# A two-layer decoder trunk on one Trainium2 core: rstd moved from the FFN's input to its outputs, one more hidden-column group as Strassen block products, and down projections issued in halves behind each group

## The chip, the cores and the metric

The kernel runs on one core of one Trainium2 chip. The metric is device time in microseconds (us), from the start of the execution to its end. The kernel before the change takes 994.29 us, the median of 3 runs that lie between 994.14 and 994.36.

Engines are named as in the profile: PE is TensorE (matrix products; PEld is its loading of the stationary operand), DVE is VectorE, ACT is ScalarE, POOL is GpSimd, and SP is SyncE, which issues most of the transfers.

## What is computed

The input is a sequence of 512 positions with 1024 channels, in float32. Two layers follow each other; each has a mixer (its own kind in each layer) and a gated FFN, both on an RMS-normalized input and added to the residual. A last RMSNorm ends the trunk. The change concerns the two FFNs:

```python
def gated_conv_ffn(x, w_gate, w_up, conv_w, conv_b, w_down):
    g = jnp.einsum('bsd,df->bsf', x, w_gate)
    g = causal_dwconv3(g, conv_w) + conv_b
    up = jnp.einsum('bsd,df->bsf', x, w_up)
    return jnp.einsum('bsf,fd->bsd', jax.nn.silu(g) * up, w_down)
...
hn = rms_norm(h, norm_ffn[layer])
h = h + gated_conv_ffn(hn, w_ffn_gate[layer], w_ffn_up[layer], ...)
```

The hidden width is 2816, so there are 22 tiles of 128 hidden columns. `rms_norm` multiplies each position by rstd, the reciprocal root of its mean square, and each channel by a gain. As rstd belongs to the position alone, it may be applied to the FFN's input or to the products of gate and up.

## The kernel before

**Number format.** Every float32 operand of a matrix product is split into two parts, hi (rounded) and lo (the rest). A product is three matmuls into one PSUM bank: hi·hi, hi·lo and lo·hi (`mm3`, L152 to 155). The split of a weight chunk costs an ACT copy (hi) and a DVE subtraction (lo) in `parts` (L145 to 150), or, in `summed` (L136 to 143), an ACT copy of the negated data into lo, an accumulating transfer issued by POOL that adds the hi/lo remainder, and another ACT copy.

**Stages.** mixer0, ffn0 (L777), mixer1 (L795), ffn1 (L1059). Channels stand on partitions and positions run along the free axis. The kernel is written for a Tile scheduler that orders the instructions of each engine by itself and allocates buffers from pools: raw weights have 4 buffers, hi and lo of weights 6 each, the tag "sum" 3, the activations 4 each, and PSUM has 7 banks for products.

**The FFN's hidden part.** The 22 tiles are worked through in groups of two (f = 0, 2, ..., 20).
- Group 0 (`direct`, L592) multiplies the weights by h times gain, which isn't normalized yet, because rstd is only being worked out beside it. `evacuate` (L609) multiplies rstd into the gate's rows (L615, DVE) and into the silu's result s (L618, POOL). It is 2 tiles × (gate, up) × 8 k-chunks × 3 = 96 matmuls of 512 columns.
- When rstd is known, `normalize` (L626) forms x = h · gain · rstd for each pair of k-chunks (L631, DVE), splits it into hi and lo again (L635 ACT, L636 DVE), and forms the block sums t23 and t41 that the block products need (L643 to L646), with their splits.
- Group 2 is direct too, on the normalized input: again 96 matmuls of 512 columns.
- Groups 4 to 20 (`both`, L681) compute gate and up with Strassen-Winograd block products: the two tiles of columns, the two halves of the 1024 channels and the two halves of the 512 positions form 2×2 blocks, and seven products replace eight. The weights' sums are s12 and s34 (L698 to L707). That is 14 products (7 for gate, 7 for up) × 4 k-chunks × 3 = 168 matmuls of 256 columns (L535). `after` (L727 and on) copies product blocks into the rows of the gate (`rows`) and into `kept` for up, or adds them there.
- Then each tile has its causal convolution (an ACT copy at L564 and two DVE SCALAR_TENSOR_TENSOR at L566), silu (L572, ACT), the product with up (L750, L751, L754, DVE) and the split into a_hi (L260, ACT) and a_lo (L262, DVE) for the down projection.

**The down projection.** `PARTS` (L516) sets the order: after groups 0 and 2 a part over tiles 0 and 1; after group 4 one over tiles 2 to 5; from there on two groups in a row and then a part over four tiles (6 to 9, 10 to 13, 14 to 17, 18 to 21), over all 1024 output columns. So each part of four tiles covers the newest group and the one before it. In layer 0 `project` (L286) does two halves of 512 output columns with the weights as stationary operand and adds into h (L305, DVE). In layer 1 `down` (L1145) has the activations as stationary operand and adds into the token-major residual y (L1109, DVE). The last part of layer 1 is followed by the final norm and the output transfers.

## Time and profile before

| what | value |
|---|---|
| median of 3 runs | 994.29 us (994.14 to 994.36) |
| the profiled execution | 994.15 us |
| its span | 992.4 us |
| granted TensorE clock, mean | 0.998 |
| instructions | 14934 |
| transfers | 125.07 MB, 126 GB/s over the span |

How to read the rows that follow in the prediction: the page's first part gives busy time, share of the span and number of instructions of each engine. A row of a group is: line, engine, operation, out<-in by name, partitions × elements and type, count | busy us, mean ns of one | idle us of the engine just before them and what ended most of it. A row of the timeline is: start, length (us), engine, line, operation, and in brackets the idle time before it with what released it. A row of the chain is: start, length, what. A row of the windows view is a stretch of the span with its length, then the busy time of each engine, the granted clock, the share of the transfer engines and GB/s. Matmuls overlap: the time that one takes from TensorE is its distance to the next one's start, and not its length.

### The profile page before, as it was taken

To read this page: it belongs to the slowest core of one execution; us is meant where nothing else is said; L and a number is where in the kernel's file an instruction comes from. 1 tells how busy PE (TensorE), PEld (TensorE's weight loads), DVE (VectorE), ACT (ScalarE), POOL (GpSimd) and SP (SyncE) were. 2 spreads that over 40 slices of the span, in tenths; PEclk is the share of its full clock that TensorE was granted. 3 is DMA by queue.
4 is the path that set the end of the run, shared out by engine and by line. 5 is a ranking of instruction groups with operands and counts; after the bars stand their busy time and mean duration, and the time that the engine had idled before them with its cause. 6 is when DMAs were issued, how large, how long until landed. Compare 5 with 4: busy or idle time off the path is not lost.

```text
span 992.4 us, 14934 instructions
## 1 busy us (share of the span) xinstructions
PE 982.9 (99%) x5905; PEld 875.6 (88%) x5905; DVE 728.5 (73%) x1104; ACT 536.3 (54%) x806; POOL 105.3 (11%) x121
## 2 busy tenths in 40 slices
PE   9999999999999999999999999999999999999997
PEld 6788888898999989999888988888989899898996
DVE  6897458967785877858988665399668768687676
ACT  5623346744653746537668634675546366363664
POOL 2141031200000000000300001211000010000100
PEclk9999999999999999999999999999999999999999
DMA  7442225544553645536423513435546456464542
GB/s 246 133 146 85 86 88 131 121 148 118 133 147 97 181 121 132 148 98 180 136 87 93 182 54 97 105 91 130 143 101 159 124 125 173 94 163 126 123 112 85
DMA packets 83073, 125.07 MB, mean 126 GB/s; under 512 B 4308, under 2 KB 56252, under 8 KB 83004
## 3 DMA queue, kind: packets, MB, share of 16 engines
q1 hardware_dynamic: 74028, 98.24, 31.4%
q0 software_dynamic: 7056, 23.60, 13.3%
q10 hardware_dynamic: 1920, 2.30, 0.7%
q8 instruction: 46, 0.75, 0.3%
q14 instruction: 23, 0.19, 0.1%
HBM read 98.42 MB, written 2.10 MB: 101 GB/s over the span
## 4 chain that ended last, share of the span: by engine, by line
PE 94%; issue 1%; DVE 1%; DMA 1%; ACT 0%; DVEq 0%; POOLq 0%; ACTq 0%
PE d L154 4%; PE d L153 4%; PE d L155 4%; PE dn L153 4%; PE dn L154 4%; PE dn L155 4%; PE gu L153 3%; PE gu L154 3%; PE gu L155 3%; PE v L153 1%; PE oo L155 1%; PE oo L153 1%; PE v L155 1%; PE oe L155 1%; PE oe L154 1%; PE v L154 1%
## 5 line engine op out<-in xcount | busy, mean ns | idle before, releaser
L153 PE MATMUL dn<-whi_dn,a_hi 128*128 128x512 f32 (+1 forms) x180 | 69.4, 386 | 0.0
L154 PE MATMUL dn<-wlo_dn,a_hi 128*128 128x512 f32 (+1 forms) x180 | 69.3, 385 | 0.0
L154 PE MATMUL d<-a_lo,whi_d 128*128 128x512 f32 x176 | 68.7, 390 | 0.0
L155 PE MATMUL d<-a_hi,wlo_d 128*128 128x512 f32 x176 | 68.5, 389 | 0.0
L155 PE MATMUL dn<-whi_dn,a_lo 128*128 128x512 f32 (+1 forms) x180 | 67.9, 385 | 0.0
L153 PE MATMUL d<-a_hi,whi_d 128*128 128x512 f32 x176 | 66.9, 390 | 0.0
L566 DVE SCALAR_TENSOR_TENSOR c<-rows,prm,c 128x512 f32<-128x512 f32 x88 | 66.4, 766 | 0.0
L141 POOL DMA_DIRECT2D wlo_g<-raw_g x22 | 19.1, 867 | 373.9 <-ACT wlo_g L140 257.9
L1109 DVE TENSOR_TENSOR y<-dn,y 128x512 f32<-128x512 f32 (+1 forms) x49 | 32.5, 674 | 23.3 <-PE dn L155 23.0
L140 ACT ACTIVATE wlo_g<-raw_g 128x1024 fp32r<-128x1024 f32 x22 | 23.2, 1056 | 42.4 <-PE dn L154 42.4
L572 ACT ACTIVATE s<-c,prm 128x512 f32<-128x512 f32 x44 | 31.7, 720 | 20.5 <-DVE c L566 20.4
L679 DVE TENSOR_TENSOR wlo_s34u<-s34u,whi_s34u 128x1024 fp32r<-128x1024 f32 x18 | 22.0, 1225 | 27.9 <-ACT whi_s34u L678 27.9
L155 PEld LDWEIGHTS dn<-whi_dn,a_lo 128*128 128x128 f32 x180 | 33.8, 188 | 7.3 <-DVE a_lo L262 0.2
L678 ACT ACTIVATE whi_s12u<-s12u 128x1024 fp32r<-128x1024 f32 x18 | 18.9, 1051 | 39.3 <-PE d L154 33.7
L153 PEld LDWEIGHTS dn<-whi_dn,a_hi 128*128 128x128 f32 x180 | 33.8, 188 | 7.0 <-ACT a_hi L260 0.2
L154 PEld LDWEIGHTS dn<-wlo_dn,a_hi 128*128 128x128 f32 x180 | 33.8, 188 | 6.4
L154 PEld LDWEIGHTS d<-a_lo,whi_d 128*128 128x128 f32 x176 | 33.1, 188 | 7.3 <-DVE a_lo L262 0.2
L305 DVE TENSOR_TENSOR h<-d,h 128x512 f32<-128x512 f32 x48 | 32.5, 683 | 9.2 <-PE d L155 9.2
L153 PEld LDWEIGHTS d<-a_hi,whi_d 128*128 128x128 f32 x176 | 32.8, 188 | 7.0
L155 PEld LDWEIGHTS d<-a_hi,wlo_d 128*128 128x128 f32 x176 | 33.0, 188 | 6.7
L260 ACT ACTIVATE a_hi<-s 128x512 fp32r<-128x512 f32 x44 | 27.6, 628 | 16.1 <-DVE s L751 7.4
L149 DVE TENSOR_TENSOR wlo_dn<-raw_dn,whi_dn 128x1024 fp32r<-128x1024 f32 x22 | 26.8, 1220 | 11.6 <-ACT whi_dn L148 11.6
(1274 smaller groups left out, 3469.1 us busy)
## 6 DMA issues: line engine op xcount, KB each, us to landing
raw_g<-in_w_ffn_gate_dram SPq DMA_DIRECT2D x36, 512.0 KB, 4.6
raw_u<-in_w_ffn_up_dram SPq DMA_DIRECT2D x36, 512.0 KB, 4.7
wlo_g<-raw_g POOLq DMA_DIRECT2D x22, 512.0 KB, 4.7
raw_d<-in_w_ffn_down_dram SPq DMA_DIRECT2D x22, 512.0 KB, 4.0
raw_dn<-in_w_ffn_down_dram SPq DMA_DIRECT2D x22, 512.0 KB, 4.0
wlo_u<-raw_u POOLq DMA_DIRECT2D x19, 512.0 KB, 4.6
raw_oe<-in_w_out_even_dram SPq DMA_DIRECT2D x8, 512.0 KB, 3.6
raw_g<-in_w_ffn_gate_dram SPq DMA_DIRECT2D x16, 256.0 KB, 2.9
```

What stands on the lines that cost most here:

```text
L140: first = nc.scalar.activation(lo, raw, AF.Copy, scale=-1.0)
L141: nc.gpsimd.dma_start(lo, raw, accum_op=ALU.add)
L149: behind(nc.vector.tensor_tensor(lo, raw, hi.bitcast(F32), ALU.subtract), after[0])
L153: nc.tensor.matmul(ps, lhs[0], rhs[0], start=start, stop=False)
L154: nc.tensor.matmul(ps, lhs[0], rhs[1], start=False, stop=False)
L155: nc.tensor.matmul(ps, lhs[1], rhs[0], start=False, stop=stop)
L260: nc.scalar.activation(hi, src, AF.Copy, scale=scale)
L305: nc.vector.tensor_tensor(h[k], ps, h[k], ALU.add)
L566: nc.vector.scalar_tensor_tensor(c, t[:, i : S + i], prm("cf", i * NF + ft), c, op0=ALU.mult, op1=ALU.add)
L572: nc.scalar.activation(s, c, AF.Silu, bias=self.prm("bf", ft))
L679: nc.vector.tensor_tensor(lo, src, hi.bitcast(F32), ALU.subtract)
L1109: nc.vector.tensor_tensor(dst, ps, dst, ALU.add)
```

## The change

The input of the FFN is no longer normalized in either layer. `normalize` is replaced by `block_sums`, which forms t23 and t41 from h times gain with no rstd in it, so it no longer waits for rstd; hg stays the un-normalized split that group 0 uses. Group 2 goes through `both` like the groups behind it. In `both`, rstd multiplies the gate's rows ahead of the convolution (DVE, in both layers), and in layer 0 also s[1] and the first two blocks of kept. In layer 1 the up half's rstd is applied in the y-add behind the down projection, as a column of four positions' scalars (`self.cols`). Group 0's multiplication of s by rstd moves from POOL to DVE in layer 0 and is dropped in layer 1.

`PARTS` gives way to `STEPS`: after group 2 comes the part of tiles 0 and 1, and after each group from 4 on half a down part, 512 output columns of a part of four tiles: behind group 4 the first half of tiles 2 to 5, behind group 6 its second half, behind group 8 the first half of tiles 6 to 9, and so on; behind group 20 both halves of tiles 18 to 21. In the steps marked late (True), the split of the group's activations is issued behind the half part. Finally `summed` takes a function `between`, with which `both` issues the split of s12 behind the negated copy and the accumulating transfer of the second weight half.

The core of the diff:

```diff
-    def summed(raw, a, b, name):
+    def summed(raw, a, b, name, between=lambda: None):
...
         first = nc.scalar.activation(lo, raw, AF.Copy, scale=-1.0)
         nc.gpsimd.dma_start(lo, raw, accum_op=ALU.add)
+        between()
         behind(nc.scalar.activation(hi, raw, AF.Copy), first)
...
-    PARTS = (((0, 2), 0, 2), ((4,), 2, 6), ((6, 8), 6, 10), ((10, 12), 10, 14),
-             ((14, 16), 14, 18), ((18, 20), 18, 22))
+    STEPS = [(0, False, []), (2, False, [(0, 2, 0), (0, 2, 1)]), (4, False, [(2, 6, 0)])]
+    for f in range(6, NF - 2, 4):
+        STEPS += [(f, True, [(f - 4, f, 1)]), (f + 2, False, [(f, f + 4, 0)])]
+    STEPS[-1][2].append((NF - 4, NF, 1))
...
+            self.cols = small[:, 3 * PAD : 3 * PAD + NT]
...
                 for j in range(2):
                     t = padded_tile()
-                    if normed:
-                        nc.scalar.copy(t[:, 2:], banks[j])
-                    else:
-                        nc.vector.tensor_tensor(t[:, 2:], banks[j], r, ALU.mult)
-                    s = self.silu(self.conv(t, f + j), f + j)
-                    if not normed:
-                        nc.gpsimd.tensor_tensor(s, s, r, ALU.mult)
+                    nc.vector.tensor_tensor(t[:, 2:], banks[j], r, ALU.mult)
+                    s = self.silu(self.conv(t, j), j)
+                    if layer == 0:
+                        nc.vector.tensor_tensor(s, s, r, ALU.mult)
...
-        def normalize(self, kp):
-
-            n, r = f"{self.layer}_{kp}", self.r
-            x = self.ap.tile([P, 2, S], F32, tag="sum", bufs=3, name=f"x{n}")
-            for i, k in enumerate((kp, kp + NP)):
-                nc.vector.scalar_tensor_tensor(x[:, i, :], h[k], self.prm("ffn", k), r,
-                                               op0=ALU.mult, op1=ALU.mult)
...
-            halves(hg[kp], x[:, 0, :])
-            halves(hg[kp + NP], x[:, 1, :])
...
+        def block_sums(self, kp):
+
+            n, g1, h1 = f"{self.layer}_{kp}", self.prm("ffn", kp + NP), h[kp + NP]
             t = self.ap.tile([P, 4, HALF], F32, tag="sum", bufs=3, name=f"t{n}")
-            nc.vector.tensor_tensor(t[:, 1, :], b22, b12, ALU.subtract)
+            b11, b12 = t[:, 2, :], t[:, 3, :]
+            nc.scalar.activation(t[:, 2:, :], h[kp].rearrange("p (a b) -> p a b", a=2), AF.Copy,
+                                 scale=self.prm("ffn", kp))
+            nc.vector.scalar_tensor_tensor(t[:, 1, :], h1[:, HALF:], g1, b12, op0=ALU.mult,
+                                           op1=ALU.subtract)
             nc.vector.tensor_tensor(t[:, 0, :], t[:, 1, :], b11, ALU.add)
-            nc.vector.tensor_tensor(t[:, 3, :], b12, b11, ALU.subtract)
-            nc.vector.tensor_tensor(t[:, 2, :], b21, t[:, 0, :], ALU.subtract)
+            nc.vector.tensor_tensor(b12, b12, b11, ALU.subtract)
+            nc.vector.scalar_tensor_tensor(b11, h1[:, :HALF], g1, t[:, 0, :], op0=ALU.mult,
+                                           op1=ALU.subtract)
...
                 w = self.unit(f"s12{key}_{n}")
-                self.halves(*w, s12)
+
+                def split_s12():
+                    self.halves(*w, s12)
+
+                hi, lo = summed(*raws[key, 1], between=split_s12)
...
-                hi, lo = summed(*raws[key, 1])
...
-                if (key, product) == ("g", 4):
-                    s[1] = self.silu(self.conv(pads[1], f + 1), f + 1)
-                elif (key, product) == ("g", 3):
-                    s[0] = self.silu(self.conv(pads[0], f), f)
+                if (key, product) in (("g", 4), ("g", 3)):
+                    j = product == 4
+                    row = pads[j][:, 2:]
+                    nc.vector.tensor_tensor(row, row, self.r, ALU.mult)
+                    s[j] = self.silu(self.conv(pads[j], f + j), f + j)
+                    if j and layer == 0:
+                        nc.vector.tensor_tensor(s[1], s[1], self.r, ALU.mult)
...
+            if layer == 0:
+                nc.vector.tensor_tensor(kept[:, :2, :], kept[:, :2, :],
+                                        self.r.rearrange("p (a b) -> p a b", a=2), ALU.mult)
...
-            elif f == 2:
-                self.direct(2, True, ((0, 1), (2, 3)), self.ch)()
             else:
-                self.both(f)
+                rows = self.both(f)
+
+            def split_acts():
+                for ft, row in rows:
+                    self.act(ft, row)
+
+            return split_acts
...
+            for f, late, down_parts in STEPS:
+                acts = ffn.hidden(f)
+                if not late:
+                    acts()
+                for a, b, half in down_parts:
...
+                    project(f"d0_{a}", w_ffn_down[0], ffn.acts, list(range(a, b)), nxt,
+                            halves=(half,))
+                if late:
+                    acts()
...
+            def add(dst, ps, t):
+                nc.vector.scalar_tensor_tensor(dst, ps, ffn.cols[:, t : t + 1], dst,
+                                               op0=ALU.mult, op1=ALU.add)
...
+            for f, late, down_parts in STEPS:
+                splits = ffn.hidden(f, before=before)
+                if not late:
+                    splits()
+                if f == NF - 2:
+                    last_down(NF - 4, NF)
+                    break
+                for part in down_parts:
+                    half_down(*part)
+                if late:
+                    splits()
```

`half_down` is the layer-1 counterpart of `project` for one half: weights of 512 output columns as the moving operand, the activations as the stationary one, and `add` at the end of each bank. `last_down` is the former last part of layer 1, with `add` for the plain addition.

120 lines of the change are left out of this document (57 added, 63 removed).

## The prediction

> **What bounds the kernel now.** I read the profile's table of engines first, then the chain that ended last.
>
> ```profile
> span 992.4 us, 14934 instructions
> ...
> PE 982.9 (99%) x5905; PEld 875.6 (88%) x5905; DVE 728.5 (73%) x1104; ACT 536.3 (54%) x806; POOL 105.3 (11%) x121
> ...
> PE 94%; issue 1%; DVE 1%; DMA 1%; ACT 0%; DVEq 0%; POOLq 0%; ACTq 0%
> ```
>
> TensorE (PE) is busy for 99% of the span, and 94% of the chain is its own work. So a change gains what it takes off TensorE's list of matmuls, and loses each microsecond for which TensorE waits for DVE, ACT or a transfer. Next I read the windows over FFN layer 0: group 0, group 2, the first down part (two tiles), group 4, and group 4's down part (four tiles).
>
> ```profile
> core 0: us, PE busy (x) PEld busy (x) DVE busy (x) ACT busy (x) POOL busy (x), PEclk, DMA share, GB/s
> 146.10:169.30 23.20, 23.20 (x109) 19.22 (x108) 17.12 (x33) 14.19 (x22) 3.98 (x4) 1.00 0.56 137
> 169.30:191.10 21.80, 21.80 (x98) 18.04 (x97) 20.58 (x34) 16.39 (x27) 6.46 (x6) 1.00 0.46 97
> 191.10:202.00 10.90, 10.90 (x50) 9.03 (x49) 10.90 (x17) 6.12 (x7) 0.87 (x1) 1.00 0.53 144
> 202.00:222.10 20.10, 20.10 (x169) 20.10 (x168) 11.41 (x17) 11.17 (x18) 0.86 (x1) 1.00 0.48 136
> 222.10:243.90 21.80, 21.80 (x98) 17.93 (x97) 18.02 (x29) 8.02 (x10) 0.86 (x1) 1.00 0.52 141
> ```
>
> No window holds idle TensorE time, at full clock (1.00). The DVE column is the one to keep: 20.58 of 21.80 us in group 2, where `normalize` runs, and all of the 10.90 us behind it. DVE is close behind TensorE here, and the change gives DVE new work.
>
> **The change part by part.**
>
> *Group 2 from direct to block products (both layers).* It removes 96 matmuls of 512 columns a layer and adds 168 of 256. Matmuls overlap, so a row's length is no price; I take start to start, by the timeline (group 2's first matmul, the first of the down part behind it) and by the chain (runs of 12 block matmuls).
>
> ```profile
> 169.32 0.39 PE L153 MATMUL gu<-hgh,whi_g 128*128 128x512 f32 x1
> ...
> 191.08 0.39 PE L153 MATMUL d<-a_hi,whi_d 128*128 128x512 f32 x1
> ...
> 203.55 1.44 PE u_4a L535 x12
> 204.99 1.44 PE g_4e L535 x12
> ```
>
> Direct: 191.08 − 169.32 = 21.76 us, or 0.2267 each. Block: 14 runs of 1.44 = 20.16 us. That is −1.60 us a layer, **−3.20 us** in all. The other matmuls stay the same in number and form; only their order changes.
>
> The Trainium skill ("TensorE: Matmul & The Clock Gate", section "Wait — 56ns, not 53.3ns?") gives start to start as columns over 2.4 GHz plus about 2.5 ns. By that page, as an estimate, the two forms cost 20.7 and 18.3 us and the gain is 2.4 us a layer, 4.7 in all. The trace has 226.7 and 120.0 ns where the page gives 215.8 and 109.2, so the trace decides.
>
> *The stall in the last group.* The largest wait on TensorE behind the first microseconds is in layer 1's group 20:
>
> ```profile
> 953.77 0.28 PE L535 MATMUL g_20a<-t,wlo_s34g 128*128 128x256 f32 x1
> 954.86 0.39 PE L535 MATMUL u_20b<-hgh,wlo_u 128*128 128x256 f32 x1 [0.81 <-DMA wlo_u<-raw_u]
> ...
> 948.88 5.94 DMA wlo_u<-raw_u
> ...
> wlo_u<-raw_u POOLq DMA_DIRECT2D x19, 512.0 KB, 4.6
> ```
>
> The gap is 954.86 − 953.77 − 0.12 = 0.97 us: the accumulating transfer that makes `wlo_u` was issued at 948.88 and took 5.94 us against a median of 4.6. Group 20 stood directly behind group 18, so its splits queued behind the rows of 18. In the new order a half down part of 10.9 us lies between every two block groups, and `between` puts the negated copy and the transfer ahead of the split of s12. Both ends: −0.97 (gone), 0 (it stays). I take **−0.97**: an issue 10 us earlier, or even 1 us earlier, clears it.
>
> *Normalizing leaves, rstd is multiplied into outputs.* Rows for each kind:
>
> ```profile
> L631 DVE SCALAR_TENSOR_TENSOR x<-h,prm,rstd_f 128x512 f32<-128x512 f32 x16 | 11.7, 743 | 4.1 <-ACT rstd_f L219 4.1
> L636 DVE TENSOR_TENSOR hgl<-x,hgh 128x512 fp32r<-128x512 f32 x16 | 10.5, 680 | 0.0
> L566 DVE SCALAR_TENSOR_TENSOR c<-rows,prm,c 128x512 f32<-128x512 f32 x88 | 66.4, 766 | 0.0
> L149 DVE TENSOR_TENSOR wlo_d<-raw_d,whi_d 128x1024 fp32r<-128x1024 f32 x22 | 26.7, 1218 | 11.6 <-ACT whi_d L148 11.6
> L305 DVE TENSOR_TENSOR h<-d,h 128x512 f32<-128x512 f32 x48 | 32.5, 683 | 9.2 <-PE d L155 9.2
> L618 POOL TENSOR_TENSOR s<-s,rstd_f 128x512 f32<-128x512 f32 x4 | 6.8, 1698 | 8.8 <-ACT s L572 8.8
> ...
> 970.03 0.69 DVE L1109 TENSOR_TENSOR y<-dn,y 128x512 f32<-128x512 f32 x1 [1.28 <-PE dn L155]
> 970.76 0.69 DVE L1117 TENSOR_TENSOR yf<-y,fin 128x512 f32<-128x512 f32 x1
> 971.37 0.68 DVE L1109 TENSOR_TENSOR y<-dn,y 128x512 f32<-128x512 f32 x1
> ```
>
> The last two starts are 0.61 us apart at 0.69 long: one DVE instruction that waits for nothing starts inside the one ahead of it. The first two are 0.73 apart, where the second reads the first's result. So a multiply of 128x512 costs 0.60 to 0.73 us. Removed per layer: 8 × 0.743 + 8 × 0.680 = 11.4 us of DVE at the entry, in windows that were 94 and 100% full. Added per block group: two multiplies of the gate's rows, and in layer 0 also s[1]·r and kept·r, so 4 × 0.61 = 2.4 us in layer 0 and 1.2 in layer 1. (The POOL multiplies of group 0, 1.70 us each, become DVE ones of 0.68.) In layer 1 the up half's rstd goes into the y-add, whose form becomes SCALAR_TENSOR_TENSOR, 0.74 against 0.685.
>
> Does a step still fit? Group 4 and its part are 11.41 + 18.02 = 29.4 us of DVE in 41.9. Half a part less (two 1.22 us splits of `wlo_d`, four 0.68 h-adds: 5.2 us) and 2.4 more makes 26.7 us in a step of 20.16 + 10.9 = 31.0: **86%**, so DVE doesn't become the bound. What can stall is the chain at a group's end. Today, behind group 8:
>
> ```profile
> 284.47 0.23 PE d L153
> ...
> 281.04 0.35 ACT L729 COPY rows<-g_8a 128x256 f32<-128x256 f32 x1
> 288.74 0.63 ACT L260 ACTIVATE a_hi<-s 128x512 fp32r<-128x512 f32 x1 [0.51 <-DVE s L754]
> ...
> 283.96 1.22 DVE L149 TENSOR_TENSOR wlo_d<-raw_d,whi_d 128x1024 fp32r<-128x1024 f32 x1
> 285.10 0.74 DVE L566 SCALAR_TENSOR_TENSOR c<-rows,prm,c 128x512 f32<-128x512 f32 x1
> ...
> 287.09 0.41 DVE L751 TENSOR_TENSOR s<-u_8a,s 128x256 f32<-128x256 f32 x1
> 287.42 0.68 DVE L679 TENSOR_TENSOR wlo_a<-raw_g,whi_a 128x512 fp32r<-128x512 f32 x1
> 288.02 0.68 DVE L754 TENSOR_TENSOR s<-kept,s 128x512 f32<-128x512 f32 x1
> 288.62 0.68 DVE L262 TENSOR_TENSOR a_lo<-s,a_hi 128x512 fp32r<-128x512 f32 x1
> ...
> 289.83 0.68 DVE L262 TENSOR_TENSOR a_lo<-s,a_hi 128x512 fp32r<-128x512 f32 x1
> ```
>
> TensorE begins the part at 284.47 with the two older tiles; 24 matmuls later (24 × 0.2267 = 5.4 us) it wants this group's `a_hi` and then `a_lo`, which end at 289.37 and 290.51. Those waits cost nothing today. In layer 0 four multiplies (2.4 us) come into this chain, so they end about 2.4 us later. In the built order of the changed kernel one product of the next group (1.44 us) and part of another stand ahead of the first matmul that reads `a_hi`, so it too comes about 2.4 us later. Adding up every DVE and ACT instruction in that order by start to start, I get `a_hi` about 0.4 us and `a_lo` about 0.2 us ahead of need; in layer 1 (two multiplies) about 0.5 us. This concerns the four steps a layer whose splits precede the half part (4, 8, 12, 16); in those marked late (6, 10, 14, 18) the half part needs only older tiles, and the slack is microseconds. Bounds for the eight: 0 to 1.4 us each (the upper end with every DVE instruction at its full length, see the first rival). I take +0.3 in all.
>
> *Layer entry.* Group 2 now follows group 0 with no wait for normalizing; `block_sums` and group 2's splits run beside group 0. By the same adding-up the tightest operand, `wlo_s12u` of group 2, is ready 0.5 us ahead of need; the removed 11.4 us of DVE is what makes this room. Bounds 0 to +1 us each; I take 0.1 each. The same for group 4, whose splits meet the chain of group 2 in a window where DVE is full today: +0.1 a layer.
>
> *Tail.*
>
> ```profile
> 985.28 0.28 PE L155 MATMUL dn<-whi_dn,a_lo 128*128 128x256 f32 x1
> ...
> 985.62 0.42 DVE L1109 TENSOR_TENSOR y<-dn,y 128x256 f32<-128x256 f32 x1
> ```
>
> The matmuls end at 985.56 and the span at 992.4; the last y-adds stand on this path and become SCALAR_TENSOR_TENSOR, some 0.06 longer each (0.743 against 0.683), of which two show: +0.1.
>
> Sum, against the profiled execution's own 994.15 us (span 992.4 and 1.75 around it; 0.14 below the median of the runs, 994.29): 994.15 − 3.20 − 0.97 + 0.3 + 0.2 + 0.2 + 0.1 = 990.78. I predict **990.8 us**; on the median the same sum gives 990.9. Against the median that is −0.35%.
>
> **The rivals.**
>
> *DVE latencies come through: slower.* If the instructions of the group-end chain don't start inside one another, each costs 0.08 us more (by the rows above 0.68 for 0.60, 0.41 for 0.33, 1.22 for 1.14). Between the gate's last multiply and `a_lo` there are some 18 in layer 0: 18 × 0.08 = 1.4 us, less 0.2 of slack, × 4 steps = 4.9 us; in layer 1 16 × 0.08 − 0.5 = 0.8, × 4 = 3.2. Time 990.8 − 0.3 + 8.1 = **998.6**; it outweighs the whole gain from about 0.05 us per instruction on (18 × 0.05 − 0.2 = 0.7 and 16 × 0.05 − 0.5 = 0.3, × 4 steps = 4.0, less the 0.3 already counted: 3.7 against a gain of 3.4). For it speaks the dependent pair 0.73 us apart; against it the independent pair 0.61 apart and the group-8 starts 287.09, 287.42, 288.02 and 288.62, which are 0.33 and 0.60 apart in the very chain that is at stake.
>
> The Trainium skill ("VectorE: DVE Perf Modes", section "Terms") says that a pipeline flush follows every DVE instruction and the next cannot issue until the pipe is empty. By that rule this rival would hold; the trace's pair 0.61 us apart at 0.69 long speaks against it.
>
> *Group 2's operands are late at both entries.* Eight block sums, eight splits and the rstd chain share DVE and ACT beside group 0. If `wlo_s12u` or t41 is 1 to 1.5 us later than I add up, each entry loses 0.5 to 1 us, and group 4 as much: 990.8 + 2 = **992.8**, about no change. For it speaks how full DVE is there today; against it the 11.4 us removed.
>
> *The transfer stays late.* If `wlo_u` still comes behind need once in the last groups, −0.97 isn't had: **991.8**.
>
> *The change doesn't bring the eighth.* Seven products for eight would be 2.7 us a layer; the rows give 1.6, since a 256-column matmul takes 0.120 and not 0.113 us. It is in the sum already.
>
> **How the numbers follow.** Forecast and its small variants, 989.6 to 992.0: 0.62. The late transfer, 991.8: 0.08. Late entries, 992 to 994: 0.16. DVE latencies, 994 to 999: 0.14, of which 0.09 over 996.3. The range 989.6 to 994.5 leaves out the upper part of the last (0.12) and a little below (0.05). A measurement here tells a difference of about 0.2% (2.0 us) from none: faster means under 992.3, slower over 996.3. Faster: 0.62 + 0.08 + a third of 0.16 = 0.75; slower: 0.09; the same: the rest, 0.16.
>
> **What would show it.** Right: 14 runs of 1.44 us in group 2 of both layers, no DMA releaser above 0.2 us ahead of u_20b, TensorE's idle rows under 1 us in the FFN, DVE near 86% in a step of layer 0. Wrong: idle TensorE ahead of the matmuls that read `a_hi` or `a_lo` in steps 4, 8, 12, 16, released by ACT or DVE (first rival); idle time in the first runs of group 2 or 4 (second); a matmul start to start other than 0.2267 and 0.120 (the main term).

## The result: 1005.86 us, 1.1% slower

The changed kernel takes 1005.86 us (median of 4 runs, 1003.32 to 1007.67) where the kernel before takes 994.21 (4 runs, 994.08 to 994.36): a ratio of 1.0114, 95% interval 1.0102 to 1.0127. The prediction was 990.8, with a range of 989.6 to 994.5. The time also became uneven: the runs of before lie within 0.3 us, those of the changed kernel within 4.4. The profiled execution is the slowest of the four, 1007.67 us, 13.5 over the profiled one of before.

### The profile after

The page of the changed kernel: its span, the engines, and the chain that ended last.

```profile
span 1006.0 us, 15310 instructions
...
PE 986.7 (98%) x6049; PEld 883.9 (88%) x6049; DVE 773.1 (77%) x1174; ACT 542.1 (54%) x816; POOL 102.4 (10%) x117
...
PE 71%; DVE 11%; DMA 6%; issue 4%; ACT 4%; POOL 1%; SPq 0%; ACTq 0%; POOLq 0%; DVEq 0%
```

TensorE's share of the chain fell from 94 to 71%, while its busy share only fell from 99 to 98%: a chain that runs through DVE, ACT and transfers tells that TensorE now waits. The 986.7 us of PE are no measure of its work, since a matmul at half clock is counted longer (0.63 us at 155.25 below, 0.39 at 150.35). So I list the waits by start to start. The timeline of TensorE, changed kernel, the matmul ahead of each larger wait and the one behind it:

```profile
150.35 0.39 PE L156 MATMUL gu<-hgh,wlo_g 128*128 128x512 f32 x1
152.65 0.27 PE L227 MATMUL ssc_f<-small,ssq_f 128*128 128x1 f32 x1 [1.91 <-POOL ssq_f L210]
...
155.25 0.63 PE L154 MATMUL gu<-hgh,whi_u 128*128 128x512 f32 x1
155.67 0.63 PE L155 MATMUL gu<-hgl,whi_u 128*128 128x512 f32 x1
...
233.56 0.28 PE L544 MATMUL u_6a<-hgl,whi_a 128*128 128x256 f32 x1
236.17 0.50 PE L154 MATMUL d<-a_hi,whi_d 128*128 128x512 f32 x1 [2.33 <-ACT a_hi L261]
...
525.58 0.39 PE L156 MATMUL v<-whi_v,hgl 128*128 128x512 f32 x1
526.50 0.50 PE L154 MATMUL v<-whi_v,hgh 128*128 128x512 f32 x1 [0.53 <-ACT v L960]
...
653.78 0.39 PE L155 MATMUL gu<-hgl,whi_g 128*128 128x512 f32 x1
655.10 0.29 PE L217 MATMUL ssr_f<-ident,rc_f1c 128*128 128x128 f32 x1 [0.93 <-DVE rc_f1c L251]
...
675.11 0.40 PE L544 MATMUL u_2e<-t,whi_s12u 128*128 128x256 f32 x2
677.63 0.39 PE L544 MATMUL u_2e<-t,wlo_s12u 128*128 128x256 f32 x1 [2.12 <-DVE wlo_s12u L679]
...
732.04 0.28 PE L544 MATMUL g_6a<-hgh,wlo_a 128*128 128x256 f32 x1
733.59 0.50 PE L154 MATMUL dn<-whi_dn,a_hi 128*128 128x512 f32 x1 [1.27 <-ACT a_hi L261]
```

A wait's price is the distance of the two starts less the pitch of the matmul ahead (0.227 us, or 0.120; 0.24 for the pair at 675.11):

| place | price, us | what it waits for |
|---|---|---|
| layer 0, sums of squares behind group 0's first matmuls | 2.07 | POOL's last addition |
| behind it, the one-column matmuls and six of 512 columns at a slower pitch | 1.95 | granted clock |
| layer 0, first half part, step 4 | 2.49 | a_hi of group 4 |
| layer 0, half parts of steps 8, 12, 16 (297.59, 360.39, 423.12) | 0.49, 0.43, 0.25 | a_hi |
| mixer1, first v group (and u_0 at 552.22: 0.45) | 0.69 | ACT's v |
| layer 1, rstd's spread in group 0 | 1.09 | DVE's rc |
| layer 1, group 2 | 2.28 | DVE's wlo_s12u |
| behind it, 256-column matmuls 0.213 us apart in place of 0.120 (678.94 to 682.35) | 1.5 | granted clock |
| layer 1, first half part, step 4 | 1.43 | a_hi of group 4 |

That is 15.1 us. Waits of 0.1 to 0.35 (groups 2 and 4, and the matmul just behind each larger wait) add about 2.5. Against it stand the 3.2 us of matmuls saved and the 0.97 us wait of u_20b, which is gone: 17.6 − 4.2 = 13.4 of the 13.5 us. The tail is 0.3 longer (from the last matmul's end, 998.81, to 1006.0: 7.2 us against 6.9), so the account is 0.2 us too large.

Eight of the table's nine rows stand at the entry of an FFN, in its first half part, or in the mixer that begins behind an FFN. The other steps lose 1.2 us together. The window from 204 to 330 us of layer 0, changed kernel (four steps):

```profile
core 0: us, PE busy (x) PEld busy (x) DVE busy (x) ACT busy (x) POOL busy (x), PEclk, DMA share, GB/s
204.00:330.00 126.00, 123.20 (x857) 115.25 (x856) 104.37 (x161) 68.01 (x99) 6.87 (x8) 1.00 0.52 138
```

DVE is busy for 104.37 of 126 us, 83%, where the prediction worked out 86. Its load isn't the limit.

### What made the operands late

**Layer 0, the entry: a queue.** Timelines of DVE and POOL, changed kernel:

```profile
146.50 1.44 DVE L679 TENSOR_TENSOR wlo_a<-raw_g,whi_a 128x512 fp32r<-128x512 f32 x1 [0.29 <-ACT whi_a L678]
147.86 0.68 DVE L310 TENSOR_TENSOR h<-oe,h 128x512 f32<-128x512 f32 x1
...
148.85 0.68 DVE L679 TENSOR_TENSOR wlo_a<-raw_u,whi_a 128x512 fp32r<-128x512 f32 x1
...
146.09 1.29 POOL L210 TENSOR_TENSOR ssq_f<-ssq_f,sq_f 128x512 f32<-128x512 f32 x1 [1.43 <-ACT sq_f L209]
149.96 2.64 POOL L210 TENSOR_TENSOR ssq_f<-ssq_f,sq_f 128x512 f32<-128x512 f32 x1 [2.57 <-DVE t L643]
```

Group 2's first split (wlo_a) now stands in DVE's queue ahead of mixer0's last addition to h, which everything in the norm waits for. That split waits 0.29 us for ACT and takes 1.44 us beside POOL's addition of 146.09, where the next split takes 0.68. So the addition to h starts 1.36 us behind group 0's first matmul (146.50); in the kernel before it starts 0.20 behind it (146.33 against 146.13). The last addition of the squares then runs on POOL beside the block sums on DVE, and takes 2.64 us where the one before it took 1.29. TensorE has 18 matmuls of group 0, 4.1 us, before it comes to that sum.

**Step 4 of both layers: a queue behind a load.** The chain of layer 0, and the timelines of DVE and ACT, changed kernel:

```profile
211.43 5.40 DMA wlo_u<-raw_u
...
217.43 4.83 DMA raw_g<-in_w_ffn_gate_dram
```

```profile
222.29 0.69 DVE L698 TENSOR_TENSOR s12g<-raw_g,raw_g 128x512 f32<-128x512 f32 x1 [3.04 <-DMA raw_g<-in_w_ffn_gate_dram]
222.90 0.69 DVE L709 TENSOR_TENSOR s34g<-raw_g 128x512 f32<-128x512 f32 x1
...
225.04 0.68 DVE L752 TENSOR_TENSOR rows<-rows,rstd_f 128x512 f32<-128x512 f32 x1
225.64 0.68 DVE L679 TENSOR_TENSOR wlo_a<-raw_g,whi_a 128x512 fp32r<-128x512 f32 x1
...
222.12 0.36 ACT L732 COPY rows<-g_4a 128x256 f32<-128x256 f32 x1
```

The accumulating transfer of group 4's wlo_u reads a raw buffer until 216.83. SP's queue of loads waits for that buffer, so raw_g of group 6 lands at 222.26. DVE's queue has group 6's s12g, which needs raw_g, ahead of group 4's rows. DVE idles 3.04 us for it. The rows are complete with ACT's copy, at 222.48; but four sums of group 6 and an addition to kept, which with the load in time would have filled the idle time, are done first, so the rows are multiplied at 225.04, and a_hi of group 4 comes about 2.5 us late. In layer 1 the same chain reads 710.08 + 5.58, 716.26 + 5.03, s12g at 721.32.

**Layer 1, group 2: buffers held by transfers.** The chain and DVE's timeline, changed kernel:

```profile
661.77 6.59 DMA t<-t
```

```profile
665.34 0.69 DVE L709 TENSOR_TENSOR s34g<-raw_g 128x512 f32<-128x512 f32 x1 [1.66 <-DMA t<-t]
...
668.55 0.69 DVE L698 TENSOR_TENSOR s12u<-raw_u,raw_u 128x512 f32<-128x512 f32 x1 [1.92 <-DMA t<-t]
```

The block sums of pairs 2 and 3 are split by accumulating transfers (t<-t), which read the tile of the sums until they land. That tile has one of the three buffers with the tag "sum" that s12 and s34 need too. So s12u of group 2 starts at 668.55. Behind it DVE's queue has group 0's rows and convolutions (672.22 to 676.44), and the split wlo_s12u, which starts at 676.35, is 2.28 us late.

### The profile page after: what moved, and what is told of

The parts are those of the page before. It is cut to its first block, busy times and chain, and to the rows that moved or that the text cites. A ratio compares the mean times of both kernels' runs of the same rounds, so it can differ in the third digit from the quotient of the medians.

```text
span 1006.0 us, 15310 instructions
## 1 busy us (share of the span) xinstructions
PE 986.7 (98%) x6049; PEld 883.9 (88%) x6049; DVE 773.1 (77%) x1174; ACT 542.1 (54%) x816; POOL 102.4 (10%) x117
## 4 chain that ended last, share of the span: by engine, by line
PE 71%; DVE 11%; DMA 6%; issue 4%; ACT 4%; POOL 1%; SPq 0%; ACTq 0%; POOLq 0%; DVEq 0%
PE dn L154 4%; PE dn L155 4%; PE dn L156 4%; PE d L154 3%; PE d L155 3%; PE d L156 3%; DMA raw_g<-in_w_ffn_gate_dram 2%; DMA wlo_u<-raw_u 2%; DVE c L578 2%; PE oo L156 1%; PE oo L154 1%; PE oo L155 1%; PE oe L155 1%; PE oe L154 1%; PE oe L156 1%
## 5 line engine op out<-in xcount | busy, mean ns | idle before, releaser
L578 DVE SCALAR_TENSOR_TENSOR c<-rows,prm,c 128x512 f32<-128x512 f32 x88 | 63.4, 743 | 0.4 <-ACT c L576 0.4
L150 DVE TENSOR_TENSOR wlo_d<-raw_d,whi_d 128x1024 fp32r<-128x1024 f32 x22 | 26.8, 1223 | 27.4 <-ACT whi_d L149 27.4
L141 POOL DMA_DIRECT2D wlo_u<-raw_u x21 | 18.1, 861 | 223.5 <-ACT wlo_u L140 137.2
L679 DVE TENSOR_TENSOR wlo_s34u<-s34u,whi_s34u 128x1024 fp32r<-128x1024 f32 x20 | 24.5, 1224 | 21.1 <-ACT whi_s34u L678 21.1
L1099 DVE SCALAR_TENSOR_TENSOR y<-dn,small,y 128x512 f32<-128x512 f32 (+1 forms) x49 | 35.6, 734 | 5.6 <-PE dn L156 5.4
L149 ACT ACTIVATE whi_dn<-raw_dn 128x1024 fp32r<-128x1024 f32 x22 | 23.3, 1058 | 29.6 <-issue 2.6
```

The lines of the kernel that those rows point to most:

```text
L141: nc.gpsimd.dma_start(lo, raw, accum_op=ALU.add)
L149: behind(nc.scalar.activation(hi, raw, AF.Copy), after[1])
L150: behind(nc.vector.tensor_tensor(lo, raw, hi.bitcast(F32), ALU.subtract), after[0])
L578: nc.vector.scalar_tensor_tensor(c, t[:, i : S + i], prm("cf", i * NF + ft), c, op0=ALU.mult, op1=ALU.add)
L679: nc.vector.tensor_tensor(lo, src, hi.bitcast(F32), ALU.subtract)
L1099: nc.vector.scalar_tensor_tensor(dst, ps, ffn.cols[:, t : t + 1], dst, op0=ALU.mult, op1=ALU.add)
```

## The experiments

Theory A, from the profile above: the loss sits where group 2's block work meets the entry of each FFN, and is made of queues and buffers there. Theory B: it is a price of every step, from the half parts (B1) or from the rstd multiplies on DVE (B2).

### Which part of the change costs it

**Group 2 direct again, the rest kept.**

```diff
+                self.ch = self.pair_weights([("g", 0), ("g", 1), ("u", 0), ("u", 1)], 2, "g")
...
+            elif f == 2:
+                rows = self.direct(self.ch, lambda i, j: None, 2, ((0, 1), (2, 3)))()
             else:
                 rows = self.both(f)
```

`pair_weights` and `direct` are made to take the group's number.

> The changed kernel with group 2 put back to direct products of 512 columns, on the un-normalized input with rstd at the evacuation; halves, rstd on outputs and block_sums stay. Theory A (the loss sits where group 2's block work meets the entry of each FFN: in the changed kernel's profile some 4.2 us around the rstd sums of layer 0, 1.2 in its groups 2 and 4, 2.6 ahead of its first down half, and 3.9 and 1.5 at the same places of layer 1, 13.4 in all): those stalls go, group 2 costs 3.2 more, about 1005.9 - 13.4 + 3.2 = 995.7. Theory B (the loss is a price of every step, from the half parts or from rstd on DVE): the stalls stay, 1005.9 + 3.2 = 1009. Half of each: about 1002.

995.52 us (10 runs, 994.59 to 995.96; ratio to before 1.001, 95% interval 1.000 to 1.0019). Theory A's number, to 0.2 us. rstd on the outputs and the half parts cost 1.1 us together against before; the rest of the 11.6 us comes with group 2's block products. In its profile step 4 has no wait, but step 12 of layer 0 has one of 1.46 us, by the same queue: s12g of the next block group waits 1.55 us for raw_g there.

**Whole parts.**

```diff
-    STEPS = [(0, False, []), (2, False, [(0, 2, 0), (0, 2, 1)]), (4, False, [(2, 6, 0)])]
+    STEPS = [(0, False, []), (2, False, [(0, 2, 0), (0, 2, 1)]), (4, False, [(2, 6, 0), (2, 6, 1)])]
     for f in range(6, NF - 2, 4):
-        STEPS += [(f, True, [(f - 4, f, 1)]), (f + 2, False, [(f, f + 4, 0)])]
-    STEPS[-1][2].append((NF - 4, NF, 1))
+        STEPS += [(f, False, []), (f + 2, False, [(f, f + 4, 0), (f, f + 4, 1)])]
```

> The changed kernel with the order of before for the down projection (two groups, then a whole part of four tiles, splits of activations always before the part). Theory A: the entries stay as they are and the time stays within 3 us of 1005.9; only what the first down part costs may move. Theory B by way of the halves: the time falls by over 5 us, to 1001 or less. The stall of 0.97 us in group 20 of layer 1 should come back.

1008.68 us (1007.12 to 1009.51; ratio 1.0141, 1.0126 to 1.0156): the entries are as slow as before the edit, so B1 falls. The wait of a_hi in step 4 went (0.11 us left): group 6's s12g stands behind group 4's chain in DVE's queue here (233.92, behind a_lo at 233.32) and no longer ahead of it, and a whole part has more matmuls of older tiles to do first than a half part. In its place u_e of groups 8, 12, 16 and 20 of layer 0 waits 0.9 to 0.96 us each for ACT's whi_s12u, and mixer1's v 2.52 us with half clock behind it. The kernel before has two groups in a row too and none of the waits of u_e, so the order alone doesn't make them; what else does is not separated. The 0.97 us of u_20b in layer 1 did not come back, against the expectation: it went without the half parts.

**The half parts alone**, on the kernel before: normalized input, group 2 direct, no rstd in the block groups. Against the changed kernel:

```diff
-                    self.block_sums(kp)
+                    self.normalize(kp)
...
-                    nc.vector.tensor_tensor(row, row, self.r, ALU.mult)
...
-                nc.vector.scalar_tensor_tensor(dst, ps, ffn.cols[:, t : t + 1], dst,
-                                               op0=ALU.mult, op1=ALU.add)
+                nc.vector.tensor_tensor(dst, ps, dst, ALU.add)
```

> The kernel before with the half parts alone (and the earlier issue of the accumulating transfer): the input is normalized, group 2 is direct on the normalized input, and no rstd on the outputs of the block groups. Theory A: no new stalls, the 0.97 us of group 20 gone: 993.2. Theory B by way of the halves: over 996.

994.09 us (10 runs, 993.49 to 995.15; ratio 0.9997, 0.9988 to 1.0007): no difference, 0.9 us above theory A's number. u_20b's wait is gone, and two waits of 0.54 and 0.36 us in steps 8 and 12 of layer 0 (0.11 of each at the matmul behind) stand against it.

**The multiplies left out.**

```diff
-                    nc.vector.tensor_tensor(row, row, self.r, ALU.mult)
...
-                        nc.vector.tensor_tensor(s[1], s[1], self.r, ALU.mult)
...
-                nc.vector.tensor_tensor(kept[:, :2, :], kept[:, :2, :],
-                                        self.r.rearrange("p (a b) -> p a b", a=2), ALU.mult)
```

> The changed kernel without the multiplications by rstd in the block groups (gate's rows in both layers, s[1] and kept in layer 0): that part of the computation is left out. It prices the multiplies. Theory A: they matter only where the chain is already late; the stalls ahead of a_hi in steps 4, 8, 12, 16 of layer 0 (2.6, 0.6, 0.5, 0.4) and step 4 of layer 1 (1.5) shrink by up to 2.4 and 1.2 us: -4 to -5, near 1001.5, and the entries' stalls stay. Theory B (rstd on DVE is the main loss): -8 or more, under 998.

1002.46 us (998.91 to 1003.81; ratio 1.0078, 1.0058 to 1.0098): 3.4 us for the multiplies of the block groups in both layers, a little less than A's 4 to 5 and far from B's 8. Its profile, taken of the fastest of the four executions (998.91), has 0.28 us of wait for a_hi left in step 4 and 0.48 at most elsewhere, the matmul behind included; the 2.07 us at layer 0's sums and the 2.29 us at layer 1's u_2e are there unchanged. B2 is a part, and not the main one.

### One cause at a time

**The order at the entry.**

```diff
-            self.added = {"g": None, "u": None}
+            self.added = {"g": norm.last_dve, "u": norm.last_dve}
...
         def halves(self, hi, lo, src):
-            nc.scalar.activation(hi, src, AF.Copy)
-            nc.vector.tensor_tensor(lo, src, hi.bitcast(F32), ALU.subtract)
+            behind(nc.scalar.activation(hi, src, AF.Copy), self.norm.last_act)
+            behind(nc.vector.tensor_tensor(lo, src, hi.bitcast(F32), ALU.subtract),
+                   self.norm.last_dve)
...
-                nc.gpsimd.tensor_tensor(self.ssq, self.ssq, sq, ALU.add)
+                e = nc.vector if self.n == NK - 1 and self.name[0] == "f" else nc.gpsimd
+                self.last_add = e.tensor_tensor(self.ssq, self.ssq, sq, ALU.add)
```

> The changed kernel with the order at the FFN's entry set: block sums and group 2's splits stand behind the last gain split (DVE) and the last square (ACT) of the norm, and the last addition of the squares is done by DVE in place of POOL, where it took 2.64 us. Theory A1 (layer 0 loses 4.2 us because DVE and ACT work for group 2 is queued ahead of the norm's last links, and the idle time then halves the clock for 3 us): the wait ahead of ssc_f and the matmuls 0.43 us apart behind it go, -3 to -4.2, to 1002 to 1003; part may come back as later operands in group 2. If the wait were owed to something else: 1005 or more.

1003.01 us (1002.07 to 1004.03; ratio 1.0089, 1.0074 to 1.0104), −2.9 against the changed kernel. TensorE's and DVE's timelines of this run:

```profile
149.93 0.39 PE L156 MATMUL gu<-hgh,wlo_g 128*128 128x512 f32 x1
150.15 0.95 PE L229 MATMUL ssc_f<-small,ssq_f 128*128 128x1 f32 x8
...
146.27 0.69 DVE L312 TENSOR_TENSOR h<-oe,h 128x512 f32<-128x512 f32 x1 [0.48 <-PE oe L156]
148.42 0.68 DVE L212 TENSOR_TENSOR ssq_f<-ssq_f,sq_f 128x512 f32<-128x512 f32 x1
```

The addition to h starts 0.20 us behind group 0's first matmul (146.07) again, the sum is ready in time, and neither the wait nor the slow matmuls are left. The edit changes two things, the order and the engine of the last addition; a run below parts them. The work that went behind the norm came back as a wait in part: u_2e of layer 0 waits 1.66 us in place of 0.27.

**Block sums without transfers.**

```diff
             for (hi, lo), src in ((self.t41[kp], t[:, 2:, :]), (self.t23[kp], t[:, :2, :])):
-                if kp < 2:
-                    self.halves(hi, lo, src)
-                    continue
-                nc.scalar.activation(lo, src, AF.Copy, scale=-1.0)
-                nc.gpsimd.dma_start(lo, src, accum_op=ALU.add)
-                nc.scalar.activation(hi, src, AF.Copy)
+                self.halves(hi, lo, src)
```

> The changed kernel with the block sums of all four pairs split by ACT and DVE, none by accumulating transfers. Theory A with the block sums' transfers (landing 6.6 us in layer 1) holding the three buffers that s12 and s34 need: the 2.4 us ahead of u_2e in layer 1 and perhaps 0.4 in layer 0 go, DVE has 2.4 us more work per layer; 1003 to 1004. If the transfers don't matter: 1006 or more.

1004.97 us (1002.34 to 1005.78; ratio 1.0101, 1.0084 to 1.0118): −0.9, less than expected and within the spread of the runs. The 2.28 us of u_2e in layer 1 are gone, as the theory says; but step 4 of layer 0 waits 3.65 us in place of 2.49 in this profile, with a stretch at half clock behind it.

**The raw buffer of groups 2 and 4 free earlier.**

```diff
-                hi, lo = summed(*raws[key, 1], between=split_s12)
+                if key == "u" and f in (2, 4):
+                    split_s12()
+                    hi, lo = parts(*raws[key, 1])
+                else:
+                    hi, lo = summed(*raws[key, 1], between=split_s12)
```

> The changed kernel with the second half of the up weights in groups 2 and 4 split by ACT and DVE, not by the accumulating transfer, so that its raw buffer is free some 4 us earlier. Theory A2 (the first down half waits because the load of the next group's raw_g waits for that buffer, and s12g, which needs the load, stands ahead of this group's rows in DVE's queue): the stalls of 2.6 and 1.5 us ahead of a_hi of group 4 shrink to under 0.7 each, -2 to -3.5, to 1002.5 to 1004; DVE has 1.1 us more work in each of the four groups. If the chain is long for its own instructions alone: 1006 or more.

1006.58 us (1004.36 to 1007.46; ratio 1.0122, 1.0107 to 1.0137): no gain in the total. The waits it aims at shrank as expected, 2.49 to 0.52 and 1.43 to 0.66. Others grew: u_4e waits 1.01 us, two in group 2 of layer 1 1.49 and 0.42, and mixer1's v 2.60 with half clock behind it. By itself this run decides nothing; the one below, with only this edit taken back, does.

**The order in mixer1.** There DVE has a subtraction on a loaded weight (raw_u) ahead of the norm's scalings.

```diff
-                    nc.vector.tensor_tensor(b12, b12, b11, ALU.subtract)
+                    behind(nc.vector.tensor_tensor(b12, b12, b11, ALU.subtract), scaled)
```

> The changed kernel with the order in mixer1 alone. By its own profile the stalls there are 0.8 and 0.55 us: 1004.5. More than 2.5 us would mean that the stalls of mixer1 vary from run to run and are larger in the other runs than in the profiled one.

1005.92 us (1004.07 to 1008.10; ratio 1.0115, 1.0102 to 1.0128): no change in the median, although the waits of v and u_0 are gone from its profile. With the runs of this kernel 4 us apart, 1.3 us can't be told here.

**The first wait filled with work.**

```diff
             ps = aux_bank(f"ssc_{self.name}")
+            if self.name == "f0":
+                for _ in range(14):
+                    order(nc.tensor.matmul(ps[:, :256], hg[0][0][:, :P], hg[0][0][:, :256],
+                                           start=True, stop=True))
```

> The changed kernel with 14 matmuls of 256 columns, whose result is overwritten, ahead of ssc_f in layer 0: 14 x 0.12 = 1.7 us of work in a wait of 2.07 us. If the matmuls 0.43 us apart behind that wait (2.9 to 5.5 us of them in the profiles of the changed kernel and of its variants) are owed to TensorE's idling: they are 0.227 apart now, the wait's end stays where it is, -1.4 to -2.7: 1003.2 to 1004.5, with a mean clock of 0.998 for that stretch's part. If the clock falls for another reason: 1005.9 or a little more.

1007.53 us (1006.84 to 1011.35; ratio 1.0145, 1.0128 to 1.0162): the total missed the expectation by 3 us. At the place itself it was met, and the slow stretch turned up elsewhere. Timeline and windows of this run:

```profile
152.14 1.05 PE L231 MATMUL ssc_f<-small,ssq_f 128*128 128x1 f32 x8 [0.27 <-POOL ssq_f L210]
...
153.37 0.40 PE L155 MATMUL gu<-hgl,whi_u 128*128 128x512 f32 x1
153.61 0.40 PE L156 MATMUL gu<-hgh,wlo_u 128*128 128x512 f32 x1
```

```profile
728.60:731.10 2.50, 0.18 (x3) 0.06 (x1) 2.50 (x4) 1.45 (x4) 0.00 (x0) 1.00 0.36 69
731.10:735.00 3.90, 3.90 (x12) 3.05 (x13) 3.37 (x5) 1.90 (x2) 0.86 (x1) 0.64 0.77 209
```

Behind the filled wait the matmuls start 0.23 us apart. Behind the wait in step 4 of layer 1, 2.48 us here, the granted clock (the figure behind POOL) is 0.64 on the mean of the second window, where the same wait of 1.43 us left it alone in the changed kernel.

### The causes together

**Entry order, block sums without transfers, and the up split of groups 2 and 4**: the three diffs above on the changed kernel.

> The order at the entry, the up split of groups 2 and 4 on DVE and the block sums without transfers, all together. If the three causes add up (4.2 + 3 + 2.4 of the 11.6 us lost): 996 to 998. If they only hide each other's waits, because DVE has 1.1 us more in each of four groups and 2.4 at each entry: over 1000.

997.13 us (8 runs, 996.71 to 999.41; ratio 1.0033, 1.0022 to 1.0044): 8.7 of the 11.6 us are recovered. The three edits alone brought 2.9, 0.9 and −0.7, which makes 3.1. They bring more together, and the profiles show why: the waits that came up behind each single edit (u_2e 1.66 us behind the first, step 4 3.65 behind the second, u_2a of layer 1 1.49 behind the third) are 0.75 us or less here. What is left is mainly mixer1, 2.50 us ahead of v and 1.6 at half clock behind it. DVE's timeline of this run:

```profile
509.72 1.22 DVE L920 TENSOR_TENSOR raw_u<-raw_u,raw_u 128x1024 f32<-128x1024 f32 x1 [4.42 <-DMA raw_u<-in_w_in_odd_dram]
510.87 1.22 DVE L150 TENSOR_TENSOR wlo_v<-raw_v,whi_v 128x1024 fp32r<-128x1024 f32 x1
512.00 1.41 DVE L872 SCALAR_TENSOR_TENSOR nx<-h,prm,rstd_m 128x512 f32<-128x512 f32 x2
```

**The same with the order in mixer1**, by the diff above (called "all" from here on).

> The run with all three mendings, and in mixer1 the first subtraction on a loaded weight (raw_u) put behind the last scaling of the norm on DVE. In that run 2.5 us of idle TensorE ahead of the first v matmuls and some 1.6 us at half clock behind it remain, because DVE waits 4.42 us for the load of raw_u with the norm's scalings queued behind it. Theory A3 (that order is the cause): 997.1 - 4 = 993, for the first time under the kernel before. If the norm itself is late: 996 to 997.

992.77 us (12 runs, 992.00 to 996.49; ratio 0.9987, 0.9979 to 0.9996): −4.4, as expected, and for the first time under the kernel before, by 0.1% (two of the 12 runs, 995.72 and 996.49, lie above it). v waits no more.

**All, but the order at the entry taken back.**

```diff
-            self.added = {"g": norm.last_dve, "u": norm.last_dve}
+            self.added = {"g": None, "u": None}
...
-            behind(nc.scalar.activation(hi, src, AF.Copy), self.norm.last_act)
+            nc.scalar.activation(hi, src, AF.Copy)
```

> All mendings but the order at the FFN's entry (the last addition of the squares stays on DVE). If POOL's 2.64 us were the cause of the 2.07 us ahead of ssc_f: the same as with all, 993. If the queue order on DVE and ACT is the cause: 1.5 to 4 us slower than with all, 994.5 to 997.

994.41 us (10 runs, 992.38 to 997.25; ratio 1.0001, 0.9992 to 1.0010): 1.6 us slower than with it. 0.71 us of wait ahead of the sums of squares are back, with the last addition on DVE (0.68 us); wlo_a stands ahead of the addition to h again and takes 1.45 us beside POOL's addition at 146.33. In the run with the block sums alone changed, where POOL makes the last addition in 1.70 us, the same wait is 1.14 us, and in the changed kernel, with 2.64, it is 2.07. So both the queue's order and POOL's slow addition make it.

**All, but the up split taken back.**

```diff
-                if key == "u" and f in (2, 4):
-                    split_s12()
-                    hi, lo = parts(*raws[key, 1])
-                else:
-                    hi, lo = summed(*raws[key, 1], between=split_s12)
+                hi, lo = summed(*raws[key, 1], between=split_s12)
```

> All mendings but the up split on DVE in groups 2 and 4: the late load ahead of s12g of group 6 comes back in both layers, 2.6 and 1.4 us: 3 to 4 us slower than with all, 996 to 997. If the earlier mendings already freed the buffer in time: the same as with all.

999.21 us (997.92 to 1000.26; ratio 1.0046, 1.0033 to 1.0059): 6.4 us slower than with it, where 3 to 4 were expected. Step 4 waits 2.71 us in layer 0 (with a slow stretch behind it) and 1.26 in layer 1. This is the second cause by itself, with the others out of the way. The third, the block sums' transfers, was not put back alone, so its share of the total is not shown.

**The up split in groups 8, 12 and 16 too.**

```diff
-                if key == "u" and f in (2, 4):
+                if key == "u" and f in (2, 4, 8, 12, 16):
```

> All mendings, and the up split on ACT and DVE in groups 8, 12 and 16 too, whose rows still make TensorE wait 0.4 to 0.6 us in layer 0. If those waits come from the late load ahead of s12g as in group 4: they go, -1 to -1.5, 991.5. If they come from DVE's load (24 to 27 of 31 us a step in layer 0): 1.1 us more of DVE work a step makes them longer, 993 to 995.

991.78 us (7 runs, 991.47 to 992.08; ratio 0.9974, 0.9963 to 0.9985): 2.6 us faster than before, and the runs lie within 0.6 us again. Its page, the start of group 2 in its chain, and its DVE timeline in step 4:

```profile
PE 979.5 (99%) x6049; PEld 880.2 (89%) x6049; DVE 786.4 (79%) x1194; ACT 528.9 (53%) x798; POOL 81.6 (8%) x97
```

```profile
169.49 1.43 PE g_2a L546 x12
170.92 1.44 PE u_2a L546 x12
```

```profile
216.60 0.69 DVE L696 TENSOR_TENSOR s12g<-raw_g,raw_g 128x512 f32<-128x512 f32 x1
...
218.42 0.69 DVE L754 TENSOR_TENSOR rows<-rows,rstd_f 128x512 f32<-128x512 f32 x1
```

DVE has more work than in the changed kernel (786.4 us against 773.1), and TensorE waits less: group 4's rows are multiplied 2.71 us ahead of the group's last matmul (218.42 against 221.13), in the changed kernel 0.67 ahead of it (225.04 against 225.70). The waits of steps 8 and 16, 0.58 and 0.40 us in the profile of the run with the split in groups 2 and 4 only, are gone although DVE has more to do, so they too came from the transfers and the loads behind them and not from DVE's load. The only waits over 0.2 us left in the FFNs are 0.59 us in group 4 of layer 0 and 0.58 in step 4 of layer 1.

**The same mendings with group 2 direct**, by the first diff of the experiments.

> All mendings, the up split in groups 4, 8, 12 and 16, and group 2 put back to direct products. If the block products of group 2 bring their 1.60 us a layer in full once their operands come in time: 991.8 + 3.2 = 995.0. If part of the gain is still lost at the entries: 993 to 994.

993.99 us (the median of ten executions from 993.01 to 994.46; an eleventh took 2519.86 us, unexplained, and isn't counted; ratio 0.9996, 0.9987 to 1.0005). So the block products of group 2 bring 993.99 − 991.78 = 2.2 us, less than the 3.2 of the expectation. In the profiles the mended kernel has 1.4 us of waits left in its FFNs (0.59 and 0.58 with 0.1 behind each), the one with group 2 direct 0.3; with these taken out the gain is 3.3 us, near the 3.2 of the sum.

## Why the prediction was wrong

**The main term was right.** Group 2 takes 14 runs of 1.44 us when its operands are there, and the gain of 3.2 us is had once the waits are mended. u_20b's 0.97 us went too, with a share of it given back in the steps by the half parts; of the two reasons given for it, the half part was not needed, since with whole parts it stayed away too. With the waits mended, by edits that the predicted kernel doesn't have, the time is 991.8, where 990.8 was predicted. The measured 1005.86 lies above every time to which the prediction gave a chance (999 at most).

**The term "layer entry" failed.** It was +0.2 for both layers, with +0.2 for group 4, and bounds of 0 to 1 us each. The runs show 2.07 + 1.95 in layer 0, 1.09 + 2.28 + 1.5 in layer 1, and 1.6 in groups 2 and 4, 10.5 us in all. The step that failed is "by the same adding-up the tightest operand, wlo_s12u of group 2, is ready 0.5 us ahead of need". It added up the instructions' durations in the built order, and left out three things that a built order has but durations don't: that an instruction on DVE holds all behind it, longer where it waits or is slowed (wlo_a ahead of the addition to h, with 0.29 us of waiting and 1.44 of its own), that a buffer is free only when the transfer that reads it has landed (the sums' t, 6.59 us), and that POOL's addition is slower beside DVE (2.64 us against 1.29). The work of the removed `normalize` was called room; but it stood behind rstd, where TensorE wasn't waiting for DVE, and the block work that replaces it stands ahead of the norm's last links.

**The term "rstd multiplies" kept its bounds in six of its eight steps, and failed in step 4.** It was +0.3 for eight steps with bounds up to 1.4 each. Steps 8, 12 and 16 of layer 0 cost 1.2 together, those of layer 1 next to nothing; but step 4 cost 2.49 and 1.43, over the upper bound of 1.4 in both. The bound was the chain at full length, with all loads in time. The load of raw_g came 3 us late, in front of the chain in DVE's queue. The prediction costed the change in work per step and not the change in when buffers come free. In step 4 the wait is absent with group 2 direct and with whole parts; the run with group 2 direct has one in step 12 instead (1.46 us), so the queue behind a load doesn't need group 2's block products.

**No term for mixer1.** The mixer cost 0.69 + 0.45 us in the profiled run, and 2.5 with 1.6 of half clock in another build. In the kernel before, the subtraction on raw_u already stands ahead of the norm's scalings and waits 2.61 us for its load, without TensorE waiting; in the changed kernel it waits 3.79 us (at 515.61), in the other build 4.42. Why the load comes later is not shown; with the half parts alone TensorE doesn't wait there. The prediction looked for effects only where the diff has lines.

**The rivals.** The first, DVE's latencies coming through, fell: the starts in the changed kernel's chain are 0.60 us apart at 0.68 long (225.04, 225.64), as in before. With it falls, for this chain, the rule of the Trainium skill ("VectorE: DVE Perf Modes", section "Terms") that the next instruction waits for an empty pipe. Its sign, idle TensorE ahead of a_hi in steps 4, 8, 12 and 16, did come in layer 0, but from late loads: it goes when they come earlier. The second, late operands at the entries, named the right place, and in layer 1 the right operand (wlo_s12u), with a chance of 0.16 and a price of 2 us; in layer 0 it was the sum of squares that came late. The price was about 10.5 us, and 4 more in the first half parts. The third, u_20b staying late, fell.

**What made it large** is that the waits hang together through the queues, with 3.4 us lost at half clock behind two of them. Mended one at a time they bring 2.9, 0.9, −0.7 and 0 us; together, with the split in groups 8, 12 and 16, they bring 14.1 (1005.86 to 991.78).

## What to carry to other kernels

On an engine that is 99% busy, ask of each instruction that moves earlier what stands behind it in its queue, and of each transfer which buffer it holds until it lands; a sum of durations in the built order is a lower bound, and slacks of half a microsecond are none. When several waits are made by one change, mend them together before judging a part: one edit alone showed no gain here and was worth 6.4 us when the others were in place.

## What the runs showed of the hardware

**The granted clock falls behind short waits, and not behind all.** Two windows of the changed kernel:

```profile
153.80:156.50 2.70, 2.70 (x7) 2.15 (x8) 2.50 (x11) 1.80 (x4) 0.00 (x0) 0.50 1.00 191
678.94:682.35 3.41, 3.41 (x19) 3.41 (x18) 3.15 (x5) 2.40 (x5) 0.00 (x0) 0.50 0.40 75
```

In the first the clock was 0.50, and 512-column matmuls started 0.43 us apart, behind a wait of 2.07 us with one-column matmuls after it. In the second it was 0.50 for 3.41 us behind the wait of 2.28 us at 675.11, and 256-column matmuls started 0.213 us apart. Behind 2.49 us at 233.56 in the same execution it stayed at 1.00. Other traces have 0.50 behind 1.14 us (the block sums alone changed, with one-column matmuls after the wait) and behind 2.71 (all, but the up split taken back), and 1.00 behind 2.80 (step 4 of layer 0 in the run with the filled wait). The Trainium skill ("TensorE: Matmul & The Clock Gate", section "What's actually happening") says that the halved clock comes after at least one idle window of about 3.4 us, and that the window runs freely and doesn't reset when a kernel starts. The trace agrees in the halving (0.50) and in the 3.41 us; but here waits of 1.14 to 2.71 us were enough some of the time. That it matters where in such a window a wait falls would fit, and is not shown. The halving fits the spread of the changed kernel's runs, whose mean clock is 0.995 to 0.998 with the slowest run at 0.995 and the fastest at 0.998.

**POOL and DVE slow each other.** At layer 0's entry POOL's addition took 2.64 us in place of 1.29, and the DVE instruction that ran beside it (first row) three times as long as the same line in layer 1 with POOL idle (second row). Earlier, beside POOL's addition at 146.09, which took 1.29 us, only DVE's wlo_a was slowed, 1.44 us in place of 0.68. DVE's timeline, changed kernel:

```profile
151.39 1.48 DVE L645 SCALAR_TENSOR_TENSOR t<-h,prm,t 128x256 f32<-128x256 f32 x1
...
650.62 0.48 DVE L645 SCALAR_TENSOR_TENSOR t<-h,prm,t 128x256 f32<-128x256 f32 x1
```

So moving one addition of a chain from POOL to DVE can take time off both: on DVE it took 0.68 us (at 148.42 in the run with the entry's order).
